# One power for two rows, the tail in another order, and the start of M1's split weights in their tiles

## The chip, the cores and the metric

The kernel runs on one core of one Trainium2 chip. The metric is device time in microseconds; the time of a kernel is the median of its runs. The engines that matter are TensorE (matrix products; the profile keeps its matmuls, PE, and its weight loads, PEld, apart), VectorE (DVE), ScalarE (ACT), GpSimd (POOL) and the DMA queues of SP, POOL and ACT.

## The reference

A decoder of two layers on 512 tokens of 1024 features, in 32-bit floats. Each layer normalises, modulates by shift and scale vectors that come from a condition vector, mixes the tokens (layer 0 with window means, layer 1 with a gated unit), adds the gated result, and then does the same with an MLP of 4096 hidden features and a squared ReLU:

```python
def rmsnorm(x, g):
    y = x * lax.rsqrt(jnp.mean(x * x, axis=-1, keepdims=True) + RMS_EPS)
    return y * g

def sq_relu_mlp(h, w1, w2):
    return jnp.square(jax.nn.relu(h @ w1)) @ w2

for i in range(DEPTH):
    sh1, sc1, g1, sh2, sc2, g2 = jnp.split(c_act @ ada_w[i] + ada_b[i], 6, axis=-1)
    h = modulate(rmsnorm(x, norm_mix_g[i]), sh1, sc1)
    y = pool_mixer(h, ...) if i == 0 else sgu_mixer(h, ...)
    x = x + g1[:, None, :] * y
    h = modulate(rmsnorm(x, norm_mlp_g[i]), sh2, sc2)
    x = x + g2[:, None, :] * sq_relu_mlp(h, mlp_w1[i], mlp_w2[i])
return rmsnorm(x, final_g)
```

## The kernel before

**Precision.** Every large product is made of three matmuls in a reduced 32-bit format: both operands are split into a high part (a copy rounded to the format) and a low part (what is left), and low x high, high x low and high x high are added up in PSUM (`mm3`, L187). `split` (L175) does this for weights: ScalarE writes the high part into a tile `wh` (L180) and VectorE the difference into a tile `wl` (L181). Both tiles come from `wpair` (L172), out of five buffers each that are used in turn. Such a tile is 1088 words long though only 1024 are used, so the used part may begin some words in: `at` is that start, in 4-byte words.

**Rows.** The 512 tokens are four row tiles t = 0 to 3 of 128 tokens. Rows 0 and 1 make up half 0, rows 2 and 3 half 1.

**The MLP.** `mlp` (L670) multiplies matrices by a scheme of seven products of half size, m = 1 to 7, in place of eight. M1, the first matmul of the MLP, is cut into units `("s", (c, j, m))`. `s_prep` (L746) fetches a block of weights, adds a second one to it where m asks for it, and splits it; `s_run` (L772) then runs 24 matmuls with 128 x 128 weights, a slice of `wh` or `wl`, and 256 moving columns, a slice of the split activations. The moving slices begin at multiples of 1024 bytes in their tiles, the weight slices at multiples of 512 bytes plus `at`. `ss_` (L744) is the list of these units in order: 42 in the first MLP (some of whose M1 is done in another way) and 56 in the second, so 98 units and 2352 matmuls. In all of them `at` is `UNDER` = 16 words, 64 bytes (L761). Everywhere else `at` is 0. M2, the second matmul, runs in units `("p", (c, m))` (`p_run`, L860) with the activations as weights and the split weights as moving operand, 512 columns at a time. The very last unit of the kernel is cut finer: row 3 is finished in two blocks of 256 columns (L887).

**Order.** TensorE's instructions are issued as the program lists them: `mlp` goes through `units`, prepares a few units ahead and runs them. On the other engines a list scheduler places the instructions at compile time, by priority (program order, with some blocks raised) and by when its model says that they are ready. Items of kind `"x"` in the list of units are calls that are made at that point.

**End of a sublayer.** `gated` (L946) multiplies a piece of the sublayer's result by the gate, adds it to the row tile `x`, squares the sum on ScalarE and keeps the sum of squares in `sums[t]`, a small tile of one row tile. With the second piece VectorE adds the two partial sums and the epsilon (L960). `rms(t)` (L964) raises that to the power -1/2 on GpSimd (`power`, L257), one instruction of 128 x 1 for each row tile. `normed(hf, i, n)` (L967) scales both row tiles of a half by these roots on ScalarE (L973), transposes them on TensorE (L985) and splits the result. It is called four times: for half 0 and half 1 ahead of layer 1's mixer, and the same ahead of layer 1's MLP. The first of these is an item of the first MLP's list, behind M2's unit (1, 4) (L1055).

**The tail.** `last1` (L1175) ends the second MLP. Rows 0, 1 and 2 are finished by `out_rows` (L1166): the power, two products of 512 columns on VectorE (L1170) and two transfers from SP's queue. Row 3 comes in three pieces; after the third its sum is completed (L962), its power taken, and its four quarters are scaled by ScalarE (L1189) and VectorE (L1191, L1192) and sent off from ACT's and SP's queues.

Of the kernel before, what the change touches and what calls it, by code (L numbers as in the profile page):

```python
# [7 lines left out]
F32 = mybir.dt.float32  # L8
F32R = mybir.dt.float32r
AF = mybir.ActivationFunctionType  # L10
ALU = mybir.AluOpType
# [3 lines left out]
P = 128  # L15
D = 1024
# [4 lines left out]
RMS_EPS = 1e-6  # L21
# [3 lines left out]

LATE = 5

UNDER = 16

LEAD = 4  # L30

# [52 lines left out]
def decoder_kernel(ctx: ExitStack, tc: tile.TileContext, xtok, vecs, rows, fgrow, ada0, adag, ada1, pool_w, w1s, w1f, w1b, w2, w_v, w_u, w_o, wsT, lnp, bs, out):  # L84
    nc = tc.nc
    V, A, G, T = nc.vector, nc.scalar, nc.gpsimd, nc.tensor
# [44 lines left out]
    def slot(tag, shape, name, dt=F32):  # L131

        pool = big if tag in ("P0", "P1", "P2", "P3", "R0", "R1", "R2", "S6", "S7") else late[0]
        return pool.tile(shape, dt, name=name, tag=tag)
# [11 lines left out]
    def X(t):  # L146
        return x_[t // 2][:, t % 2]
# [27 lines left out]
    def split(r, n=1, at=0):  # L175

        h, l = wpair(at)
        for q in range(n):
            c = slice(D // n * q, D // n * (q + 1))
            A.activation(h[:, c], r[:, c], AF.Copy)  # L180
            V.tensor_tensor(l[:, c], r[:, c], f32(h[:, c]), ALU.subtract)  # L181
        return h, l
# [74 lines left out]
    def power(v, n):  # L257

        r = sm.tile([P, n], F32, name="rr", tag=f"rr{n}")
        G.tensor_tensor(r, v, mhalf[:, 0:n], ALU.pow)  # L260
        return r
# [8 lines left out]
    with (  # L270
# [67 lines left out]
        def rms():  # L338
            v0 = sm.tile([P, NT], F32, name="rv4", tag="rv4")
            V.tensor_scalar(v0, ss, RMS_EPS, None, ALU.add)  # L340
            rt.append(power(v0, NT))
# [328 lines left out]
    def mlp(i, extra, units, final):  # L670
# [75 lines left out]
        def s_prep(u):  # L746
            c, j, m = u

            def b(r, n):
                return blk(c, j, r, n)  # L750

            def add(o, r, n):
                G.dma_start(o, w1b[i, 2 * c + j, r, n], accum_op=ALU.add)

            t = b(0, 0)
            if m in (5, 6):
                V.tensor_tensor(t, t, b(*CHAIN[m]), ALU.add)
            if m == 5:
                add(b(0, 1), 1, 1)
            wb = b(1, 1) if m == 3 else b(1, 0) if m == 2 else b(0, 1) if m == 7 else t  # L760
            w = split(wb, 1, UNDER)  # L761
            if m == 6:
                add(t, *CHAIN[4])
            for at in more.get(u, ()):
                blk(*at)
            if spare and (u == ss_[0] or in_gb(c, j, *{2: (1, 0), 3: (1, 1)}.get(m, (0, 0)))):
                blk(*spare[0])
            return w
# [177 lines left out]
    def gated(t, c0, n, src, y=None):  # L946
        tmp = sm.tile([P, S], F32, name="tmp", tag="tmp", bufs=2)[:, 0:n]
        xt = X(t)[:, c0 : c0 + n]
        if y is not None:
            V.tensor_tensor(y, y, src, ALU.add)  # L950
        V.tensor_tensor(tmp, src if y is None else y, gbs[0][:, c0 : c0 + n], ALU.mult)
        V.tensor_tensor(xt, xt, tmp, ALU.add)  # L952
        if t not in sums:
            sums[t] = sm.tile([P, 4], F32, name="sums", tag=f"sums{t}", bufs=1), []
        s, cs = sums[t]
        A.activation(tmp, xt, AF.Square, scale=D**-0.5, accum_out=s[:, len(cs) : len(cs) + 1])  # L956
        cs.append(c0)
        if len(cs) == 2:

            V.tensor_scalar(s[:, 3:4], s[:, 0:1], s[:, 1:2], RMS_EPS, ALU.add, ALU.add)  # L960
        elif len(cs) == 3:
            V.tensor_tensor(s[:, 3:4], s[:, 3:4], s[:, 2:3], ALU.add)  # L962

    def rms(t):  # L964
        return power(sums.pop(t)[0][:, 3:4], 1)

    def normed(hf, i, n):  # L967

        xs = []
        x2 = slot(f"R{hf}", [P, 2, D], "xs") if n else None  # L970
        for r in range(2):
            t = x2[:, r] if n else w4.tile([P, D], F32, name="xs", tag="w4")
            A.activation(t, X(2 * hf + r), AF.Copy, scale=rms(2 * hf + r))  # L973
            xs.append(t)
        c = slice(256 * hf, 256 * hf + 256)
        if (i, n, hf) == (1, 0, 0):
            h_[:] = hparts(["S0", "S1", "S2", "S3"])
        if (i, n, hf) == (1, 1, 0):
            h32[:] = [slot(f"P{j}", [P, 4, S], "h32") for j in range(2)]
            h_[:] = hparts(["S0", "S1", "S2", "S3"])  # L980
        for k in range(0, KD, 2):
            px = bank("px")
            for q in range(2):
                for r in range(2):
                    T.transpose(px[:, 256 * q + P * r : 256 * q + P * r + P], xs[r][:, P * (k + q) : P * (k + q) + P], ident)  # L985
            tt = h32[k // 4][:, k % 4 : k % 4 + 2, c] if i and n else sm.tile([P, 2, 256], F32, name="tt", tag="tmp", bufs=2)
            for q in range(2):
                a, b = scl[i][n][:, k + q : k + q + 1], mod(i, c_sh(n, k + q))
                if q or n:
                    A.activation(tt[:, q], px[:, 256 * q : 256 * q + 256], AF.Identity, bias=b, scale=a)  # L990
                else:
                    V.tensor_scalar(tt[:, q], px[:, 0:256], a, b, ALU.mult, ALU.add)
            if (i, n, hf) != (1, 1, 1):
                parts(H2(k, c), tt)
# [27 lines left out]
    def after(us, at, *what):  # L1022
        n = us.index(at) + 1
        us[n:n] = what
# [27 lines left out]
    us += rest(2, 0)  # L1052
    after(us, ("s", (3, 1, 3)), ("tl", (0,)))
    us += p_units(((3, 2), 0, 0), ((3, 2), 1, 0), ((1, 4), 2, 1), ((1, 4), 3, 1))
    after(us, ("p", (1, 4)), ("x", lambda: normed(0, 1, 0)))  # L1055
    after(us, ("p", (1, 5)), ("x", spread(0, "gain0")))
    mlp(0, ex, us, lambda t, dh, c0, n, src, y: gated(t, S * dh + c0, n, src, y))

# [105 lines left out]
        nc.sync.dma_start(fgb[0], fgrow.rearrange("(o a) -> o a", o=1).to_broadcast([P, D]))  # L1164

    def out_rows(t):  # L1166
        r = rms(t)
        for j in range(2):
            c = slice(S * j, S * j + S)
            V.scalar_tensor_tensor(X(t)[:, c], X(t)[:, c], r, fgb[0][:, c], ALU.mult, ALU.mult)  # L1170
            nc.sync.dma_start(out[t, :, j], X(t)[:, c])
# [3 lines left out]
    def last1(t, dh, c0, n, src, y):  # L1175
        gated(t, S * dh + c0, n, src, y)
        done.append(t)
        if t < NT - 1:
            if done.count(t) == 2:
                out_rows(t)  # L1180
            return
        xt = X(t)
        if done.count(t) == 1:
            V.tensor_tensor(xt[:, S:D], xt[:, S:D], fgb[0][:, S:D], ALU.mult)
        elif done.count(t) == 2:
            V.tensor_tensor(xt[:, 0:256], xt[:, 0:256], fgb[0][:, 0:256], ALU.mult)
        else:
            r = rms(t)
            A.activation(xt[:, S:D], xt[:, S:D], AF.Copy, scale=r)  # L1189
            nc.scalar.dma_start(out[t, :, 1], xt[:, S:D])  # L1190
            V.scalar_tensor_tensor(xt[:, 256:S], xt[:, 256:S], r, fgb[0][:, 256:S], ALU.mult, ALU.mult)  # L1191
            V.tensor_scalar(xt[:, 0:256], xt[:, 0:256], r, None, ALU.mult)  # L1192
            nc.sync.dma_start(out[t, :, 0], xt[:, 0:S])
# [102 lines left out]
```

## Time and profile before

| | |
|---|---|
| three timed runs | 858.62, 863.02 and 864.4 us; median 863.02 |
| profiled execution | 864.85 us, span 863.1 us, mean granted TensorE clock 0.992 |
| instructions | 12746 |
| M1 of the first MLP | about 106 to 226 us |
| M2 of the first MLP | about 226 to 387 us |
| layer 1's mixer | about 387 to 534 us |
| M1 of the second MLP | 534 to 700 us |
| M2 of the second MLP and the tail | 700 to 863 us |

The span runs from the first to the last instruction of the program on the core. In the rows of a view, `out<-in` are tiles by their names in the program, `x` is the count, and what stands in brackets is the engine's idle time before the instruction with the instruction that ended it. A matmul's end is modelled, so the distance from one start to the next says more than its length. Rows of the chain of waits follow the work that ended last back to the start.

### The profile page before, as it was taken

To read this page: it belongs to the slowest core of one execution; us is meant where nothing else is said; L and a number is where in the kernel's file an instruction comes from. 1 tells how busy PE (TensorE), PEld (TensorE's weight loads), DVE (VectorE), ACT (ScalarE), POOL (GpSimd) and SP (SyncE) were. 2 spreads that over 40 slices of the span, in tenths; PEclk is the share of its full clock that TensorE was granted. 3 is DMA by queue.
4 is the path that set the end of the run, shared out by engine and by line. 5 is a ranking of instruction groups with operands and counts; after the bars stand their busy time and mean duration, and the time that the engine had idled before them with its cause. 6 is when DMAs were issued, how large, how long until landed. Compare 5 with 4: busy or idle time off the path is not lost.

```text
span 863.1 us, 12746 instructions
## 1 busy us (share of the span) xinstructions
PE 836.9 (97%) x4895; PEld 737.4 (85%) x4895; DVE 690.0 (80%) x878; ACT 514.9 (60%) x740; POOL 117.9 (14%) x137
## 2 busy tenths in 40 slices
PE   9999999999999999989999999999999999999995
PEld 7878898999978888768888887989999998888884
DVE  6889888988689868786799954788787677976886
ACT  4286776666665655656331436867766676665562
POOL 3010001000133300032010001011000032321000
PEclk9999999999999999989999999999999999999998
DMA  9999868899999989344758733558989699998502
GB/s 350 406 339 325 252 186 238 262 284 276 302 217 173 204 224 253 138 163 169 243 180 292 237 121 104 155 155 195 271 245 259 172 220 245 196 214 221 155 17 82
DMA packets 51652, 188.62 MB, mean 219 GB/s; under 512 B 5740, under 2 KB 5892, under 8 KB 50567
## 3 DMA queue, kind: packets, MB, share of 16 engines
q1 hardware_dynamic: 37090, 133.52, 42.9%
q0 software_dynamic: 14352, 54.02, 32.7%
q8 instruction: 38, 0.62, 0.3%
q10 hardware_dynamic: 148, 0.27, 0.1%
q14 instruction: 24, 0.19, 0.1%
HBM read 181.49 MB, written 6.30 MB: 218 GB/s over the span
## 4 chain that ended last, share of the span: by engine, by line
PE 58%; DVE 19%; DMA 12%; issue 5%; ACT 4%; POOL 1%; SPq 0%; POOLq 0%; DVEq 0%; ACTq 0%
PE pm L874 28%; PE po L193 6%; DVE wl L181 4%; DVE ada L217 3%; PE b211q L193 3%; PE b301q L193 3%; DMA wh<-in_ada 2%; PE b201q L193 2%; PE b311q L193 2%; DMA ada<-in_ada 2%; DVE ada L397 2%; ACT wh L180 1%; PE b111q L193 1%; PE b205q L193 1%; PE b305q L193 1%
## 5 line engine op out<-in xcount | busy, mean ns | idle before, releaser
L874 PE MATMUL pm<-wh,o 128*128 128x512 f32 x864 | 216.1, 392 | 3.8 <-DVE o L638 3.1
L874 PEld LDWEIGHTS pm<-wh,o 128*128 128x128 f32 x864 | 162.4, 189 | 39.6 <-DVE o L638 4.3
L874 PE MATMUL pm<-wl,o 128*128 128x512 f32 x432 | 115.7, 389 | 0.1
L180 ACT ACTIVATE wh<-bt 128x1024 fp32r<-128x1024 f32 x64 | 67.1, 1057 | 51.8 <-PE pm L874 42.1
L874 PEld LDWEIGHTS pm<-wl,o 128*128 128x128 f32 x432 | 81.0, 188 | 17.4 <-DVE wl L181 0.5
L181 DVE TENSOR_TENSOR wl<-bt,wh 128x1024 fp32r<-128x1024 f32 x64 | 77.5, 1218 | 20.1 <-ACT wh L180 20.1
L638 DVE TENSOR_TENSOR o<-g,o 128x1024 fp32r<-128x1024 f32 x56 | 68.2, 1217 | 5.6 <-ACT o L637 5.5
L217 DVE SCALAR_TENSOR_TENSOR ada<-ada,cb 128x1024 f32<-128x1024 f32 x56 | 68.0, 1217 | 3.5 <-DMA ada<-in_ada 3.1
L193 PE MATMUL po<-hb,wh 128*128 128x512 f32 x224 | 69.0, 389 | 0.0
L637 ACT ACTIVATE o<-g 128x1024 fp32r<-128x1024 f32 x56 | 58.7, 1048 | 9.5 <-PE pm L874 8.8
L180 ACT ACTIVATE wh<-b 128x1024 fp32r<-128x1024 f32 x32 | 34.0, 1062 | 37.6 <-PE pm L874 37.6
L853 POOL DMA_DIRECT2D bt<-in_w x48 | 41.5, 894 | 108.6 <-DVE wl L181 86.7
L181 DVE TENSOR_TENSOR wl<-b,wh 128x1024 fp32r<-128x1024 f32 x32 | 39.2, 1224 | 21.3 <-ACT wh L180 21.3
L180 ACT ACTIVATE wh<-raw 128x1024 fp32r<-128x1024 f32 x33 | 35.0, 1060 | 32.8 <-PE pm L874 13.8
L181 DVE TENSOR_TENSOR wl<-raw,wh 128x1024 fp32r<-128x1024 f32 x33 | 40.2, 1221 | 14.3 <-ACT wh L180 14.2
L193 PEld LDWEIGHTS po<-hb,wh 128*128 128x128 f32 x224 | 42.1, 188 | 8.6
L193 PE MATMUL po<-hb,wl 128*128 128x512 f32 x112 | 44.1, 394 | 0.5 <-ACT g L700 0.5
L692 ACT ACTIVATE g<-g 128x512 f32<-128x512 f32 (+1 forms) x72 | 41.2, 601 | 1.2
L193 PE MATMUL po<-wh,gt 128*128 128x512 f32 x128 | 40.5, 393 | 0.3 <-DVE gt L1137 0.2
L193 PE MATMUL po<-wh,hb 128*128 128x512 f32 x128 | 39.9, 390 | 0.0
L797 ACT ACTIVATE g<-g 128x512 f32<-128x512 f32 x42 | 26.2, 624 | 16.1 <-DVE g L789 8.7
L956 ACT ACTIVATE tmp<-x 128x512 f32<-128x512 f32 (+1 forms) x25 | 15.2, 609 | 26.9 <-DVE x L952 26.9
(442 smaller groups left out, 2027.6 us busy)
## 6 DMA issues: line engine op xcount, KB each, us to landing
ada<-in_ada SPq DMA_DIRECT2D x72, 512.0 KB, 4.7
bt<-in_w POOLq DMA_DIRECT2D x48, 512.0 KB, 9.0
bt<-in_w SPq DMA_DIRECT2D x16, 512.0 KB, 6.1
raw<-in_w SPq DMA_DIRECT2D x16, 512.0 KB, 7.1
b<-in_w SPq DMA_DIRECT2D x16, 512.0 KB, 10.0
b<-in_w POOLq DMA_DIRECT2D x16, 512.0 KB, 10.2
wh<-in_ada SPq DMA_DIRECT2D x9, 512.0 KB, 9.9
wl<-in_ada SPq DMA_DIRECT2D x9, 512.0 KB, 10.1
```

Of the source, the lines that this page charges most:

```text
L180: A.activation(h[:, c], r[:, c], AF.Copy)
L181: V.tensor_tensor(l[:, c], r[:, c], f32(h[:, c]), ALU.subtract)
L193: T.matmul(o[:, c], a, b[:, c], start=first and q == 0 and not c.start, stop=last and q == 2 and c.stop is None, **kw)
L217: keep(V.scalar_tensor_tensor(r, r, 1.0, cb, ALU.mult, ALU.mult, accum_out=pmv[i, b][:, j : j + 1]))
L397: V.scalar_tensor_tensor(r, r, 1.0, cb, ALU.mult, ALU.mult, accum_out=out)
L637: A.activation(o[0], a, AF.Copy)
L638: V.tensor_tensor(o[1], a, f32(o[0]), ALU.subtract)
L692: A.activation(t, t, AF.Square)
L797: A.activation(t, t, AF.Relu)
L853: G.dma_start(r, piece(c, *nxt, q), accum_op=ALU.add)
L874: T.matmul(banks[hf], o[a][:, 2 * q + p, hf], w[q][b][:, S * p : S * p + S], start=start and q + n + p == 0, stop=stop and q + n + p == 4, ...
L956: A.activation(tmp, xt, AF.Square, scale=D**-0.5, accum_out=s[:, len(cs) : len(cs) + 1])
```

## The change

**M1's weights.** `UNDER` becomes a tuple, and unit number n of a list takes entry n modulo 7 for both of its tiles: the used part begins 64, 128, 192, 32, 96, 160 or 0 bytes into the tile.

**One power for two rows.** The partial sums of both row tiles of a half lie in one tile `[P, 2, 4]`. `roots(hf)` adds the two partial sums and the epsilon of both rows in one VectorE instruction and takes one power of 128 x 2. Ahead of layer 1's MLP (`one=True`) it keeps a sum and a power for each row, in a tile they share. The sums are no longer added up in `gated` but where the roots are taken. For half 0 ahead of layer 1's mixer the roots are called for behind M2's unit (0, 4) and not in `normed` behind unit (1, 4).

**The tail.** Row 2's `out_rows` is called after row 3's power, and the last of row 3's three squares is made by VectorE in place of ScalarE.

```diff
-UNDER = 16
+UNDER = (16, 32, 48, 8, 24, 40, 0)
...
-            w = split(wb, 1, UNDER)
+            w = split(wb, 1, UNDER[ss_.index(u) % len(UNDER)])
...
-        if t not in sums:
-            sums[t] = sm.tile([P, 4], F32, name="sums", tag=f"sums{t}", bufs=1), []
-        s, cs = sums[t]
-        A.activation(tmp, xt, AF.Square, scale=D**-0.5, accum_out=s[:, len(cs) : len(cs) + 1])
+        pair, cs = sums.setdefault(t // 2, (sm.tile([P, 2, 4], F32, name="sums", tag=f"sums{t // 2}", bufs=1), ([], [])) if t // 2 not in sums else None)
+        s, cs = pair[:, t % 2], cs[t % 2]
         cs.append(c0)
-        if len(cs) == 2:
-
-            V.tensor_scalar(s[:, 3:4], s[:, 0:1], s[:, 1:2], RMS_EPS, ALU.add, ALU.add)
-        elif len(cs) == 3:
-            V.tensor_tensor(s[:, 3:4], s[:, 3:4], s[:, 2:3], ALU.add)
-
-    def rms(t):
-        return power(sums.pop(t)[0][:, 3:4], 1)
-
-    def normed(hf, i, n):
+        o = s[:, len(cs) - 1 : len(cs)]
+        if len(cs) == 3:
+            V.scalar_tensor_tensor(tmp, xt, 1.0 / D, xt, ALU.mult, ALU.mult, accum_out=o)
+        else:
+            A.activation(tmp, xt, AF.Square, scale=D**-0.5, accum_out=o)
+
+    def total(t):
+        s = sums[t // 2][0][:, t % 2]
+        V.tensor_scalar(s[:, 3:4], s[:, 0:1], s[:, 1:2], RMS_EPS, ALU.add, ALU.add)
+        return s
+
+    def roots(hf, one=False):
+        pair = sums.pop(hf)[0]
+        v = sm.tile([P, 2], F32, name="rv", tag="rv2")
+        if one:
+            r = sm.tile([P, 2], F32, name="rr", tag="rr2")
+            for q in range(2):
+                V.scalar_tensor_tensor(v[:, q : q + 1], pair[:, q, 0:1], RMS_EPS, pair[:, q, 1:2], ALU.add, ALU.add)
+                G.tensor_tensor(r[:, q : q + 1], v[:, q : q + 1], mhalf[:, 0:1], ALU.pow)
+            return r
+        V.scalar_tensor_tensor(v, pair[:, :, 0], RMS_EPS, pair[:, :, 1], ALU.add, ALU.add)
+        return power(v, 2)
+
+    def normed(hf, i, n, rr=None):
 
         xs = []
+        rr = roots(hf, n == 1) if rr is None else rr()
...
-            A.activation(t, X(2 * hf + r), AF.Copy, scale=rms(2 * hf + r))
+            A.activation(t, X(2 * hf + r), AF.Copy, scale=rr[:, r : r + 1])
...
-    after(us, ("p", (1, 4)), ("x", lambda: normed(0, 1, 0)))
+    rr = []
+    after(us, ("p", (1, 4)), ("x", lambda: normed(0, 1, 0, rr.pop)))
+    after(us, ("p", (0, 4)), ("x", lambda: rr.append(roots(0))))
...
-        r = rms(t)
+        r = power(total(t)[:, 3:4], 1)
...
-            if done.count(t) == 2:
+            if done.count(t) == 2 and t < 2:
                 out_rows(t)
...
             V.tensor_tensor(xt[:, 0:256], xt[:, 0:256], fgb[0][:, 0:256], ALU.mult)
+            total(t)
         else:
-            r = rms(t)
+            s = sums[1][0][:, 1]
+            V.tensor_tensor(s[:, 3:4], s[:, 3:4], s[:, 2:3], ALU.add)
+            r = power(s[:, 3:4], 1)
+            out_rows(2)
             A.activation(xt[:, S:D], xt[:, S:D], AF.Copy, scale=r)
```

## The prediction

> **What bounds the kernel now.** I read the page first, for the busiest engine and the chain; then the chain in order of time; then TensorE's timeline inside M1, the first matmul of both MLPs; then the windows of M1's two long stretches; last the places that the small edits touch.
>
> ```profile
> PE 836.9 (97%) x4895; PEld 737.4 (85%) x4895; DVE 690.0 (80%) x878; ACT 514.9 (60%) x740; POOL 117.9 (14%) x137
> PE 58%; DVE 19%; DMA 12%; issue 5%; ACT 4%; POOL 1%; SPq 0%; POOLq 0%; DVEq 0%; ACTq 0%
> ```
>
> TensorE is busy for 97% of the span and carries 58% of the chain that ended last. So the question is how fast it works where it never waits.
>
> ```profile
> 187.08 2.83 PE b211q L193 x24
> 267.32 73.50 PE pm L874 x324
> 697.27 2.83 PE b311q L193 x24
> ```
>
> These are rows of the chain in order of time: start, length, matmuls. One M1 unit (`s_run`) is 24 matmuls with 256 moving columns, 2.83 us or 117.9 ns each; from 150 to 222 us and from 576 to 699 us nearly every piece of the chain is such a unit, one behind the other. A matmul of M2 with 512 columns takes 73.50 / 324 = 226.9 ns, so half of it would be 113.4 ns for 256 columns. M1 is some 4 ns above that, and M1 is where the weights' start is changed. The same timeline shows that M1 has two speeds:
>
> ```profile
> 125.78 0.39 PE L193 MATMUL b101q<-hb,wl 128*128 128x256 f32 x1
> 138.25 0.28 PE L193 MATMUL b115q<-as,wl 128*128 128x256 f32 x1
> 140.97 0.28 PE L193 MATMUL b111q<-hb,wl 128*128 128x256 f32 x1
> 147.24 0.39 PE L193 MATMUL b111q<-hb,wl 128*128 128x256 f32 x1 [0.67 <-DVE g L793]
> 150.17 0.28 PE L193 MATMUL b205q<-as,wl 128*128 128x256 f32 x1
> 153.00 0.28 PE L193 MATMUL b201q<-as,wl 128*128 128x256 f32 x1
> 558.95 0.36 PE L193 MATMUL b112q<-hb,wl 128*128 128x256 f32 x1
> 569.14 0.38 PE L193 MATMUL b001q<-as,wl 128*128 128x256 f32 x1 [1.62 <-DVE wl L181]
> 572.63 0.38 PE L193 MATMUL b011q<-as,wl 128*128 128x256 f32 x1 [0.48 <-DVE wl L181]
> ```
>
> Each row is the first matmul of a unit. From 138.25 to 140.97 a unit takes 2.72 us, 113.3 ns a matmul; from 150.17 to 153.00 the same work takes 2.83 us, 117.9 ns. The fast speed begins behind an interruption at 125.78, ends behind one at 147.24, returns about 559 and ends at 572.63; between interruptions it doesn't change. That is 11 of the 98 units (42 in the first MLP, 56 in the second). It isn't a matter of buffers or operands: the seven units from 125.78 to 147.24 go round all five weight buffers, and both kinds of moving operand (`hb`, `as`) occur at both speeds. It is a phase between two streams, the weights that are loaded for the next matmul and the columns that move through the present one, and it stays until something breaks it. The granted clock is 1.00 at both speeds:
>
> ```profile
> 136.00:146.00 10.00, 10.00 (x91) 10.00 (x90) 8.34 (x10) 5.05 (x8) 0.86 (x1) 1.00 0.93 290
> 152.00:222.00 70.00, 70.00 (x596) 70.00 (x596) 63.88 (x85) 47.70 (x64) 6.04 (x7) 1.00 0.90 281
> 576.00:699.00 123.00, 123.00 (x1047) 123.00 (x1046) 94.50 (x103) 85.33 (x116) 12.98 (x15) 1.00 0.84 232
> ```
>
> (Length, PE, PEld, DVE, ACT and POOL busy, clock, DMA share, GB/s.) In the first MLP VectorE is busy for 63.88 of 70 us and the DMA engines for 90%; in the second VectorE for 94.50 of 123. A dearer matmul lands on the end in both; a cheaper one in full only in the second.
>
> **The change part by part.**
>
> *M1's weight starts.* The tuple has seven starts, and 42 and 56 units are 6 and 8 rounds of it, so each start serves 14 units. Moving operands begin at whole kilobytes of their tiles and weight blocks at 512-byte steps plus the start. Today all of M1 is at 64 bytes. The only other place with 256 moving columns in this arithmetic is the last block of the last unit, where both operands have start 0:
>
> ```profile
> 850.48 0.28 PE L193 MATMUL pm<-wl,o 128*128 128x256 f32 x1
> 851.56 0.28 PE L193 MATMUL pm<-wl,o 128*128 128x256 f32 x1
> ```
>
> Nine matmuls lie between these two: 1.08 / 9 = 120.0 ns. So start 0 is 2.1 ns dearer than start 64 at its slow speed. The other five starts have no row; the bounds are 113.3 and 120.0, and further up a rival. I take 128 like 0 (both whole steps of 128 bytes) at 120.0, and 192 like 64 at 117.9. For 32, 96 and 160 I take 117.9, the row of a start that is out of step too. Mean: (5 x 117.9 + 2 x 120.0) / 7 = 118.5. Today's mean: (11 x 113.3 + 87 x 117.9) / 98 = 117.4. The difference of 1.1 ns on 98 x 24 = 2352 matmuls is +2.6 us, all of it on the path. With the three half steps at either bound it is -2.0 or +4.7 us; ScalarE's and VectorE's writes to the shifted tiles keep their length, and should one grow, they wait on TensorE in both stretches.
>
> The Trainium skill speaks against any effect: "SBUF — State Buffer", section "Who interferes with whom", gives TensorE two independent read ports, one for the moving operand and one for weights, and says that PE never waits on anyone. By it the start of the weights costs nothing and this term is 0; the two speeds of one and the same unit, 113.3 and 117.9 ns, don't fit it.
>
> *One power for two rows, before the second layer's first norm.*
>
> ```profile
> L260 POOL TENSOR_TENSOR rr<-sums,mhalf x12: 538/556/4886, 369.5 to 857.4; 128x1 f32<-128x1 f32 x12
> 369.32 1.21 DVE L181 TENSOR_TENSOR wl<-bt,wh 128x1024 fp32r<-128x1024 f32 x1
> 369.48 5.42 POOL L260 TENSOR_TENSOR rr<-sums,mhalf 128x1 f32<-128x1 f32 x2 [42.40 <-DVE sums L960]
> 371.59 2.35 DVE L181 TENSOR_TENSOR wl<-bt,wh 128x1024 fp32r<-128x1024 f32 x2
> 374.40 2.19 ACT L973 ACTIVATE xs<-x,rr 128x1024 f32<-128x1024 f32 x2 [3.95 <-POOL rr L260]
> 375.61 0.47 PE L985 MATMUL px<-ident,xs 128*128 128x128 f32 x1 [2.35 <-ACT xs L973]
> 376.65 3.46 PE L985 MATMUL px<-ident,xs 128*128 128x128 f32 x15 [0.57 <-ACT xs L973]
> ```
>
> A power takes 0.54 to 0.56 us, but the first of this pair took 4.89: it began at 369.48 and ended, with VectorE's unbroken run of tensor-tensor work (369.32 to 373.94), at 374.37. ScalarE waited 3.95 us, TensorE 2.35 + 0.57. This is the stall that the earlier call aims at. But row 1's sum, which the joint power needs, still comes behind ScalarE's second square, in the same place of VectorE's queue (about 369.2), and the second power is not what is waited for: it ended about 374.9 while ScalarE worked on row 0 until 375.5. The joint power would again sit under VectorE's run and end about 374.4. I put it at 0: the power is held by VectorE, not by its own place. Bounds: -2.9 us if it finds a gap before the run, +0.6 if the sum slips behind the run (a sum, 0.2, and the handing over). The same page and section of the skill names that lock: a VectorE instruction with two SBUF inputs contends with a GpSimd one that reads SBUF, and the later one blocks; the trace agrees, 4.89 us against 0.54.
>
> In the other norms two short sums become one, or are made later: 0.21 us of VectorE each (the sum's row in the next fence), on no path that TensorE waits for longest. I cost them at 0; the queue behind them on VectorE is the splits of the next units, which can come 0.2 us earlier or later.
>
> *The tail.*
>
> ```profile
> 852.83 0.21 DVE L960 TENSOR_SCALAR sums<-sums 128x1 f32<-128x1 f32 x1
> 853.76 1.41 DVE L1170 SCALAR_TENSOR_TENSOR x<-x,rr,fgb 128x512 f32<-128x512 f32 x2 [0.72 <-POOL rr L260]
> 855.55 0.41 DVE L951 TENSOR_TENSOR tmp<-pm,gb 128x256 f32<-128x256 f32 x1
> 856.52 0.42 ACT L956 ACTIVATE tmp<-x 128x256 f32<-128x256 f32 x1 [3.04 <-DVE x L952]
> 857.06 0.16 DVE L962 TENSOR_TENSOR sums<-sums 128x1 f32<-128x1 f32 x1 [0.64 <-ACT tmp L956]
> 857.94 0.48 DVE L1191 SCALAR_TENSOR_TENSOR x<-x,rr,fgb 128x256 f32<-128x256 f32 x1 [0.72 <-POOL rr L260]
> 858.35 0.35 DVE L1192 TENSOR_SCALAR x<-x,rr 128x256 f32<-128x256 f32 x1
> 858.72 0.33 SPq L1193 DMA_DIRECT2D out<-x  x1
> ```
>
> Row 2's two products (1.41 us) stand ahead of row 3's last gate at 855.55. If they really move behind row 3's power, the gate starts about 1.3 us earlier, but VectorE has the same work before it is done: what it loses in front it does at the end, and row 2's own two transfers leave SP's queue there, with row 3's behind them. Only the wait for GpSimd (0.72) could be filled: -0.7 us. Against that, four transfers instead of two leave in the last 1.5 us; I allow +0.5. The third square on VectorE instead of ScalarE costs about 0.48 (the 256-column product's row) plus reading the sum, against 0.62 from 856.44 to the sum at 857.06: -0.1. Together -0.1, between -0.8 and +0.5.
>
> *Sum.* +2.6 + 0 + 0 - 0.1 = +2.5 us. The profiled execution took 864.85 us (span 863.1), so 867.35; it lies 1.8 us above the median of the three timed runs, 863.02. On the median's footing: 865.5 us. A difference under 1% (8.6 us) I call no change, which is about what a measurement here can tell.
>
> **The rivals.**
>
> *The change of start breaks the phase (faster).* Of the five interruptions quoted above three left it fast (125.78, 558.95, 569.14) and two slow (147.24, 572.63): about half. If a new start at each unit acts as an interruption does, without its wait, 49 units are fast instead of 11: 38 x 24 x 4.6 ns = 4.2 us. About 1 us of it is lost in the first MLP, whose VectorE is already at 91% and which waited 0.67 us at the end of its fast stretch. -3.3 us: 859.7. It decides as soon as more than some 35 units run fast, for then it outweighs the 2.6 us above. For it: the speed depends on nothing but history. Against: start 0 gave 120.0 in the tail from its first matmuls, so a start has a speed of its own.
>
> *All starts but 64 are free of the conflict (faster).* 87 x 24 x 4.6 ns = 9.6 us, less 1 in the first MLP: 854.5. Against it: the tail.
>
> *Half steps cost double (slower).* A weight block that begins at 32, 96 or 160 bytes may touch one more step of memory and meet the moving columns twice as often. The tail's excess over the fast speed is 6.7 ns; doubled, 126.7 for three starts of seven: mean 122.3, +4.9 ns, +11.5 us: 874.5. Nothing in the trace speaks for or against it.
>
> *The start does nothing.* The speed depends on history alone, and 113.3, 117.9 and 120.0 come from other things than starts; then the small edits are left: 863 us, where the skill's rule of two free ports would put it. The tail's 120.0 is against it.
>
> **How the numbers follow.** Forecast 0.45 (865.5), phase broken 0.22 (859.7), nothing 0.15 (863), half steps double 0.10 (874.5), all free 0.08 (854.5). The likeliest gives the time. 857 to 870.5 leaves out the last two, and takes in the bounds of the half steps (861 to 867.6), of the power (-2.9) and of the tail around the first three. Faster by over 1% (under 854.4) is half of "all free" and a little of the phase: 0.06. Slower by over 1% (over 871.7) is "half steps double" and the upper end of the forecast: 0.10. Within: 0.84.
>
> **What would show it.** In the timeline of the changed kernel the first matmuls of M1's units lie 2.83 us apart for starts 64 and 192 and 2.88 for 0 and 128; the half steps show their own price. Rows of 2.72 in more than 35 units mean the phase rival; 2.72 nearly everywhere, the all-free one; 3.0 at three starts of seven, the doubled one. The first power still ends with VectorE's run, about 5 us after it starts, and TensorE still waits about 2.9 us there. Row 2's two products lie behind row 3's last gate, and the last transfer leaves right behind the last product, as it does now. I am wrong if the M1 term has the other sign, or if the stall at the power goes.

## The result, and the profile after

The changed kernel takes 865.87 us (median of 11 runs, 863.62 to 869.35); the kernel before, run beside it on the same chips, 860.85 us (11 runs, 853.36 to 866.81). The ratio is 1.008, 95% interval 1.0054 to 1.0105: no change by the bound of 1%, and a loss all the same, as the interval lies above 1. The two profiled executions don't show that loss: 863.62 us after, the changed kernel's lowest run, against 864.85 us before, one of the highest of before. The difference between these two traces is therefore not the difference between the kernels, and much of what follows is about that.

Two lines of the page after, engine totals and chain shares:

```profile
PE 836.3 (97%) x4895; PEld 736.8 (85%) x4895; DVE 690.2 (80%) x878; ACT 514.3 (60%) x738; POOL 115.8 (13%) x135
PE 77%; DVE 9%; DMA 7%; issue 3%; ACT 3%; POOL 1%; SPq 0%; DVEq 0%; POOLq 0%; ACTq 0%
```

TensorE is still what the time consists of, now with 77% of the chain against 58%. The chain in order of time (start, length, group, matmuls) shows M1's units one behind the other, so that each one's speed can be read off:

```profile
160.24 2.87 PE b201q L193 x24
163.12 2.86 PE b211q L193 x24
165.98 2.83 PE b201q L193 x24
168.81 2.85 PE b215q L193 x24
171.66 2.83 PE b211q L193 x24
174.48 2.84 PE b215q L193 x24
177.32 2.82 PE b212q L193 x24
180.14 2.87 PE b211q L193 x24
```

The weights of these eight begin 160, 0, 64, 128, 192, 32, 96 and again 160 bytes into their tiles; a row's length divided by 24 gives 119.6, 119.2, 117.9, 118.8, 117.9, 118.3, 117.5 and 119.6 ns a matmul. Over all units (the mean time between the starts of a unit's consecutive matmuls, without the few distances over 150 ns, which hold a wait; a unit is called fast below 115 ns) M1 takes 118.3 ns with 3 units below 115, against 117.3 with 11 in the trace of before: 2352 x 0.93 ns = 2.2 us between the two traces. Next, windows (length, then PE, PEld, DVE, ACT and POOL busy with counts, clock, DMA share, GB/s): of before a stretch of layer 1 in which most matmuls have 512 columns, and of after the first MLP's stretch, which the prediction showed of before, and the same stretch of layer 1:

```profile
412.00:442.00 30.00, 30.00 (x134) 24.85 (x133) 26.11 (x42) 9.74 (x12) 2.00 (x2) 1.00 0.69 223
```

```profile
152.00:222.00 70.00, 70.00 (x593) 70.00 (x592) 63.68 (x84) 48.00 (x64) 6.64 (x8) 1.00 0.89 278
412.00:442.00 30.00, 30.00 (x131) 24.33 (x130) 27.57 (x46) 9.29 (x13) 2.84 (x3) 1.00 0.71 237
```

In the first stretch 593 matmuls fit where 596 did. The second was not in the prediction at all: TensorE never waits in these 30 us and the clock is 1.00 in both, yet three matmuls fewer fit. Their starts say why: 480 matmuls of 512 columns now lie 232.5 ns apart on average, where the others, and all of them before, lie 227.0 apart.

The stall at the second layer's first norm, after (the timeline there: start, length, group, and in brackets the wait before it and its releaser):

```profile
369.04 3.90 POOL L260 TENSOR_TENSOR rr<-rv,mhalf 128x2 f32<-128x2 f32 x1 [43.35 <-DVE rv L976]
370.01 2.35 DVE L181 TENSOR_TENSOR wl<-bt,wh 128x1024 fp32r<-128x1024 f32 x2
372.97 2.19 ACT L986 ACTIVATE xs<-x,rr 128x1024 f32<-128x1024 f32 x2 [3.94 <-POOL rr L260]
374.17 0.33 PE L998 MATMUL px<-ident,xs 128*128 128x128 f32 x1 [2.45 <-ACT xs L986]
375.21 3.03 PE L998 MATMUL px<-ident,xs 128*128 128x128 f32 x13 [0.71 <-ACT xs L986]
```

One power for both rows, 3.90 us instead of 4.89; it began 1.1 us nearer to the end of VectorE's run (372.36 here) and again ends just behind it. ScalarE waits 3.94 us (3.95 before), TensorE 2.45 + 0.71 (2.35 + 0.57 before). And the tail:

```profile
853.27 0.43 DVE L951 TENSOR_TENSOR tmp<-pm,gb 128x256 f32<-128x256 f32 x1
854.19 0.42 DVE L958 SCALAR_TENSOR_TENSOR tmp<-x 128x256 f32<-128x256 f32 x1
854.96 1.05 POOL L260 TENSOR_TENSOR rr<-sums,mhalf 128x1 f32<-128x1 f32 x2 [16.36 <-DVE sums L1205]
856.05 1.41 DVE L1185 SCALAR_TENSOR_TENSOR x<-x,rr,fgb 128x512 f32<-128x512 f32 x2 [1.24 <-POOL rr L260]
857.38 0.48 DVE L1210 SCALAR_TENSOR_TENSOR x<-x,rr,fgb 128x256 f32<-128x256 f32 x1
857.77 0.35 DVE L1211 TENSOR_SCALAR x<-x,rr 128x256 f32<-128x256 f32 x1
858.15 0.33 SPq L1212 DMA_DIRECT2D out<-x  x1
```

Row 3's last gate now stands right behind the last matmul, and row 2's products behind row 3's power, as the change says.

### The profile page after: what moved, and what is told of

Its sections match the earlier page's. It is cut to its first block, busy times and chain, and to the rows that moved or that the text cites. A ratio compares the mean times of both kernels' runs of the same rounds, so it can differ in the third digit from the quotient of the medians.

```text
span 861.9 us, 12735 instructions
## 1 busy us (share of the span) xinstructions
PE 836.3 (97%) x4895; PEld 736.8 (85%) x4895; DVE 690.2 (80%) x878; ACT 514.3 (60%) x738; POOL 115.8 (13%) x135
## 4 chain that ended last, share of the span: by engine, by line
PE 77%; DVE 9%; DMA 7%; issue 3%; ACT 3%; POOL 1%; SPq 0%; DVEq 0%; POOLq 0%; ACTq 0%
PE pm L874 30%; PE po L193 17%; DVE wl L181 3%; PE b211q L193 3%; PE b201q L193 3%; PE b301q L193 3%; PE b311q L193 3%; DMA wh<-in_ada 2%; PE b111q L193 2%; PE b101q L193 1%; PE b315q L193 1%; PE b305q L193 1%; PE b215q L193 1%; PE b205q L193 1%; PE pm L193 1%
## 5 line engine op out<-in xcount | busy, mean ns | idle before, releaser
L193 PEld LDWEIGHTS po<-wh,hb 128*128 128x128 f32 x128 | 24.1, 188 | 5.6
```

Source lines behind the costliest of these rows:

```text
L193: T.matmul(o[:, c], a, b[:, c], start=first and q == 0 and not c.start, stop=last and q == 2 and c.stop is None, **kw)
```

## The experiments

Each was run against the kernel before on the same chip. A table first, of every trace: M1's mean time per matmul and how many of its 98 units are below 115 ns; the time per matmul of the 480 matmuls of 512 columns whose operands the small edits move; whether the granted clock falls in 370 to 385 us and in 485 to 505 us; the profiled run's time, and the median with its number of runs.

| kernel | M1 ns (fast units) | 512 columns, ns | falls | profiled us | median us (runs) |
|---|---|---|---|---|---|
| before | 117.3 (11) | 227.0 | 1st | 864.85 | 860.85 (11), 859.66 over all 100 |
| before_again | 117.1 (16) | 226.9 | both | 866.50 | one run |
| before_third | 114.2 (80) | 227.0 | 1st | 854.87 | one run |
| before_fourth | 114.1 (81) | 227.0 | both | 857.29 | one run |
| after | 118.3 (3) | 232.5 | 1st | 863.62 | 865.87 (11) |
| small_edits | 116.4 (32) | 232.6 | none | 860.97 | 861.05 (12) |
| starts_turn | 118.3 (3) | 227.0 | both | 869.46 | 865.26 (12) |
| start96 | 117.5 (0) | 232.6 | none | 864.58 | 865.17 (12) |
| small_aligned | 115.7 (46) | 227.0 | both | 862.74 | 859.73 (12) |
| before_shifted | 116.0 (41) | 232.6 | none | 860.15 | 860.82 (12) |
| after_aligned | 118.4 (1) | 227.0 | 1st | 862.10 | 866.14 (10) |
| start192 | 117.8 (0) | 227.0 | both | 869.69 | 867.01 (9) |
| starts_fine | 118.5 (0) | 227.0 | both | 866.28 | 866.51 (10) |
| two_starts | 113.9 (86) | 227.0 | both, and at 230 to 250 us | 865.70 | 857.80 (12) |

### The change taken apart: small edits alone, starts alone

The changed kernel with all starts at 64 bytes:

```
-UNDER = (16, 32, 48, 8, 24, 40, 0)
+UNDER = (16,)
```

> The change with all M1 starts back at 64 bytes, so the joint power and the new tail alone. Theory A (the loss is M1's: the turning starts cost the fast speed of 113.3 ns that before has in stretches): the time is that of before, 0 to -1 us (the profiled tail of the change is 0.8 us shorter, from the last matmul to the last transfer), ratio 0.998 to 1.001, and M1 again has stretches at 113.3 ns. Theory B (the small edits cost it): +4 to +6 us, ratio 1.005 to 1.008, with M1's pitch as before.

The kernel before with only the starts turning:

```
-UNDER = 16
+UNDER = (16, 32, 48, 8, 24, 40, 0)
...
-            w = split(wb, 1, UNDER)
+            w = split(wb, 1, UNDER[ss_.index(u) % len(UNDER)])
```

> The kernel before with only the seven starts in turn. Theory A: as the whole change, ratio 1.006 to 1.010, mean M1 pitch 118.2 to 118.5 ns, at most 5 units of 98 at 113.3. Theory B: the M1 part alone would be at most the difference of the two profiled executions' means, 118.3 - 117.3 = 1.0 ns x 2352 = 2.2 us, ratio 1.002 to 1.003.

The changed kernel with all starts at 96 bytes:

```
-UNDER = (16, 32, 48, 8, 24, 40, 0)
+UNDER = (24,)
```

> The change with all M1 starts at 96 bytes, the cheapest of the new starts in the change's trace (116.6 to 118.5 ns by unit, mean 117.2). If a start has a speed of its own: M1 at 116.6 to 117.2 throughout, 1 ns under the slow speed of 64; against before, which has part of its units at 113.3, ratio 0.999 to 1.004. If the speed is a matter of history alone: M1 as in before, both speeds, 113.3 and 117.8.

And the kernel before once more, for its trace:

> The kernel before once more, for its profile. Theory A says that its spread (853 to 867 us) is the number of units at the fast speed: time = 864.9 - 0.108 x (fast units - 11), so an execution at 860 us has about 55 fast units. Theory C (the spread comes from transfers or waits): the number of fast units stays near 11 and the waits of TensorE differ.

The small edits alone: ratio 1.0024 (0.9996 to 1.0052), above theory A's range and below theory B's. The turning starts alone: 1.0049 (1.002 to 1.0077), 865.26 against 860.24 us, between the two theories in time, with M1 as theory A said (118.3 ns, 3 fast units). So by the medians the larger part of the loss is M1's. Start 96 for all units: 1.0061 (1.0034 to 1.0088), above what was expected, with no fast unit, so history alone doesn't set the speed; yet its M1 mean of 117.5 ns is hardly above that of the first trace of before. That is the first sign that 117.3 ns is not what before usually has. The second is the spread: before runs from 854.96 to 866.6 us here, start96 only from 862.91 to 867.57. The second trace of before, 866.50 us, has 16 fast units and two falls of the clock where the first has one, so it decides between neither of its theories.

### Where the tiles lie

The small edits change more than their instructions. Four small tiles of sums (32 bytes each in the allocation) became two, and two new names for pairs of values came with three buffers each: 6 x 32 - 2 x 32 = 128 bytes more, and every tile behind them moved by as much. Among these are all four tiles that hold `hb` in the second layer and two of the four that hold `gt`; the weight tiles `wh` and `wl` lie in front and stayed. Before, both operands of every 512-column matmul of this line began at the same place modulo 256 bytes; after, 480 of them are 128 bytes apart. An unused tile of 128 bytes tells this from the joint power:

```
     sums = {}
+    sm.tile([P, 32], F32, name="pad", tag="pad", bufs=1)
```

Added to the kernel before it moves the tiles by 128 bytes; added to the change it makes the move 256 bytes in all, so the places modulo 256 are those of before. It went into the small edits alone, into the kernel before, and into the whole change:

> The changed kernel with every weight start at 64 bytes (the small edits alone) and one unused tile of 128 bytes among the small tiles. In the traces of the three kernels with the joint power, the new small tiles have moved the tiles named hb and two of the four named gt by 128 bytes, and the 480 matmuls of 512 columns that read them together with an unmoved weight tile take 232.4 to 232.8 ns where the others take 227.0. The unused tile brings them back to the places of before. Theory L (the cost follows where the tiles lie): those matmuls fall back to 227.0 ns, 480 x 5.5 ns = 2.6 us less than the small edits alone (861.05 us): 858.4 us, 0.998 of before. Theory P (the cost follows the moment at which TensorE starts again behind the joint power): the 232 ns stay, and the time stays at 861.0 us. Theory B (other work of the small edits costs it): the time stays at 861.0 us although the matmuls take 227.0 ns.

> The kernel before, with one unused tile of 128 bytes among its small tiles and nothing else, so that hb and two of the gt tiles begin 128 bytes later, as in the changed kernel. Theory L: the 480 matmuls of 512 columns go from 227.0 to 232.5 ns, +2.6 us: 862.8 us, 1.003 of before; of M1's units, those that read the moved tiles have their weights 192 instead of 64 bytes away, which the rows of the small edits price at nothing (117.8 ns both). Theory P: no joint power, so no cost: 860.2 us, and 227.0 ns throughout.

> The changed kernel with its seven starts, and the unused tile of 128 bytes that brings hb and gt back to the places of before. Theory L: 865.9 - 2.6 = 863.3 us, 1.0035 of before, what is left being M1's turning starts; M1's mean is 118.4 ns as in the kernel that has the turning starts alone. Theory P: 865.9 us. If the turning starts were the whole loss (theory A), the time would stay at 865.3 us whatever the tiles' places.

The stretch of 512-column matmuls in before_shifted, and then in small_aligned:

```profile
412.00:442.00 30.00, 30.00 (x131) 24.32 (x130) 26.86 (x48) 8.08 (x10) 4.85 (x4) 1.00 0.69 227
```

```profile
412.00:442.00 30.00, 30.00 (x134) 24.86 (x133) 27.02 (x48) 8.09 (x10) 4.62 (x4) 1.00 0.69 233
```

131 matmuls with the tiles moved and no joint power, 134 with the joint power and the tiles back. As to the matmuls theory L is shown, and P falls: the 232.6 ns follow the tiles' places, at a price of 480 x 5.5 ns = 2.6 us. As to the time it is not shown. before_shifted, 1.0016 (0.9987 to 1.0044), lies 1.2 us above before, and small_aligned, 0.9999 (0.9964 to 1.0034), 1.3 us below the small edits, each half of what L said and within the noise; after_aligned, 1.0074 (1.0045 to 1.0104), is no faster than the changed kernel.

Two things in the traces give time back. One is a wait of TensorE for VectorE's `gt`, here in before_again:

```profile
493.50 0.80 PE L193 MATMUL po<-wh,gt 128*128 128x512 f32 x1 [3.15 <-DVE gt L1137]
```

From the first matmul that reads `hb` to the first that reads `gt` takes 96.1 us in the ten traces with the tiles in their old places and 98.2 us in the four with moved tiles. TensorE so comes later to `gt` and waits less: its waits from there on add up to 0 to 3.85 us in the ten, 2.2 in the mean, and to 0 to 0.7 us in the four, 0.2 in the mean. From the first matmul with `hb` to the last with `gt` all 14 traces take 141.4 to 148.1 us, the ten 145.1 in the mean and the four 144.6, so in them nothing is left of the 2.6 us at the end of this stretch, though with this scatter that isn't shown for the kernels. The other is the clock. The windows behind the stall, before and then small_edits:

```profile
375.00:380.00 5.00, 3.83 (x17) 3.54 (x18) 2.10 (x3) 4.32 (x6) 0.00 (x0) 0.55 0.65 213
380.00:385.00 5.00, 5.00 (x19) 4.00 (x19) 5.00 (x8) 3.40 (x8) 0.00 (x0) 0.77 0.75 225
```

```profile
375.00:380.00 5.00, 4.63 (x28) 4.14 (x29) 4.05 (x6) 4.28 (x7) 0.00 (x0) 1.00 0.71 261
380.00:385.00 5.00, 5.00 (x23) 4.13 (x23) 5.00 (x8) 3.34 (x6) 1.81 (x1) 1.00 0.88 302
```

Behind TensorE's wait the granted clock fell to 0.55 and 0.77 in one trace, which costs (0.45 + 0.23) x 5 = 3.4 us of TensorE's work, and not at all in the other. Of the ten traces with the tiles in their old places all have this fall, and seven have the second one, at 485 to 505 us; of the four with moved tiles one has the first and none the second. Over all runs the mean granted clock is 0.9941 with the tiles moved (47 runs) and 0.9927 otherwise (154 runs, the difference 0.0014 with a standard error of 0.0004): 0.0014 x 860 = 1.2 us given back. The second fall comes in the seven traces in which the waits for `gt` add up to 2.17 us or more, and in no other, so for this one the shorter wait is the likely reason. The first fall depends on how its wait lies in time. All changes of the clock in one trace are whole multiples of 3.41 us apart, and a fall lasts 3.41 or 6.83 us. Here are such steps of 3.41 us, before and then small_edits:

```profile
372.06:375.47 3.41, 1.19 (x6) 0.65 (x4) 1.88 (x2) 1.07 (x2) 2.85 (x2) 1.00 0.21 19
375.48:378.88 3.40, 2.71 (x12) 2.42 (x13) 0.98 (x2) 2.72 (x5) 0.00 (x0) 0.50 0.74 294
```

```profile
370.00:373.40 3.40, 1.89 (x9) 1.23 (x7) 2.52 (x3) 0.27 (x1) 3.09 (x1) 1.00 0.00 0
373.42:376.82 3.40, 1.78 (x14) 1.60 (x15) 0.87 (x2) 3.07 (x4) 0.00 (x0) 1.00 0.86 307
```

In before most of the wait falls into one step, with TensorE busy for 1.19 us, and the next step has half the clock; in the small edits nearly the same wait is shared by two steps, and the clock stays. Between 12 and 840 us of the 14 traces every step at full clock with TensorE busy for at most 1.53 us (20 of them) is followed by half the clock, and none of the 3331 with 1.64 us or more is. Nothing in the traces ties the place of the steps to that of the tiles, so that three of the four traces with moved tiles escape the first fall may be chance. That after_aligned shows no gain fits its clock (0.9919 against 0.9935 of the changed kernel, 1.4 us) and the scatter of ten runs; its time alone doesn't show the 2.6 us.

The Trainium skill, page "TensorE: Matmul & The Clock Gate", Part 1, describes such a gate: half rate is the default, activity lifts it, and an idle window of about 3.4 us brings it back. The lowest clock in a row here is 0.50, which agrees; but a step of 3.41 us need not be idle to bring it, as TensorE was busy for up to 1.53 us of such a step.

### Is 192 the other side of 64?

```
-UNDER = 16
+UNDER = 48
```

> The kernel before with every weight start at 192 bytes instead of 64. In the traces so far a unit of start 64 takes 113.3 or 117.8 ns per matmul, in stretches, and in one stretch of the small edits (from 574 us on) units 64 bytes away are fast while units 192 bytes away are slow. Theory T (the two starts are the two sides of one phase: where 64 is slow, 192 is fast): the 82 to 87 units that are slow in before become fast and its 11 to 16 fast ones slow, some 70 x 0.108 = 7.6 us less: 852.6 us. Theory A (192 has the same two speeds and falls into the slow one for most units): 117.5 ns in the mean, 860 to 861 us, no difference from before.

867.01 us, 1.0085 (1.0052 to 1.0119), the dearest of all. No unit was fast, 98 of 98 lie at 117.6 to 117.9 ns. Theory T falls. Theory A's M1 mean of 117.5 was right, its time wrong by 6 us, because it compared with a trace of before that had few fast units itself.

### Neighbours of 64

```
-UNDER = (16, 32, 48, 8, 24, 40, 0)
+UNDER = (12, 14, 18, 20, 4, 28, 44)
```

> The kernel before with M1's weight starts turning unit by unit through 48, 56, 72, 80, 16, 112 and 176 bytes, so that each start's price shows in 14 units; the prices so far, in ns per matmul: 0 bytes 119.3, 32 118.3, 64 113.3 or 117.8, 96 117.5, 128 118.7, 160 119.9, 192 117.8 and never fast. Theory S (each start has a price of its own, and the turning breaks nothing): neighbours of 64 share its two speeds, so 56, 72 or 80 have some units near 113.3, the others lie between 117.3 and 120; the time is 2352 x (mean of the rows - 116.2) above before, some 862 to 866 us. Theory R (only the 64-byte cell of the start counts): 72, 80 and 112 take 113.3 or 117.8 as 64 does, 16, 48 and 56 take 119.3 as 0 does, 176 takes 118.7 as 128 does: mean 118.2, 864.5 us. Theory A (the turning itself holds every start out of its fast speed): no unit below 115.

866.51 us, 1.0078 (1.0041 to 1.0114). The means by start: 16 bytes 118.5, 48 118.2, 56 117.8, 72 118.5, 80 118.7, 112 119.9, 176 118.2; no unit below 117.5. Theory R falls with start 112, in the same 64 bytes as 64 and the dearest of all. Theory S fails with the neighbours 56, 72 and 80, none of which shares the fast speed. Theory A's forecast came true, but this run alone doesn't show that the turning is the cause: these starts may be slow by themselves.

### What an ordinary execution of before looks like

Two more traces of the kernel before:

> The kernel before, once more, for its trace: does a lower time come with more of M1's units at 113.3 ns? The two traces of before so far have 11 and 16 such units of 98 and mean clocks of 0.992 and 0.991, at 864.85 and 866.5 us, which are among its highest times. Theory F (two states that change from run to run make its spread: the share of M1 at 113.3 ns, 0.108 us a unit, and the dips of the granted clock behind the waits near 372 and 490 us, some 0.86 us for each 0.001 of the mean clock): time = 864.85 - 0.108 x (fast units - 11) - 0.86 x (clock - 0.992)/0.001, within 2 us; at the median of 860 us that is some 25 to 40 fast units, or a clock near 0.996. Theory C (transfers make the spread): the fast units stay at 11 to 16 and the clock at 0.991 or 0.992, whatever the time.

> As the run beside it, one more trace of the kernel before: theory F gives its time within 2 us from its fast units and its clock, 864.85 - 0.108 x (fast units - 11) - 0.86 x (clock - 0.992)/0.001; theory C expects 11 to 16 fast units at any time.

The first MLP's stretch and one of the second MLP's, before_third:

```profile
152.00:222.00 70.00, 70.00 (x620) 70.00 (x619) 65.10 (x88) 48.01 (x65) 6.90 (x8) 1.00 0.90 288
580.00:680.00 100.00, 100.00 (x884) 100.00 (x884) 80.18 (x87) 72.54 (x101) 9.53 (x11) 1.00 0.84 240
```

and the second one in the trace of before that the prediction was made from:

```profile
580.00:680.00 100.00, 100.00 (x851) 100.00 (x850) 81.16 (x89) 70.51 (x96) 10.39 (x12) 1.00 0.84 234
```

620 matmuls where the prediction quoted 596, 884 where it would have found 851, with the same program. The chain of before_fourth says the same by units:

```profile
134.50 2.72 PE b111q L193 x24
137.22 2.72 PE b115q L193 x24
139.94 2.72 PE b111q L193 x24
```

80 and 81 units are fast, against 11 and 16. Theory F's formula gives 864.85 - 0.108 x 69 - 0.86 x 2 = 855.7 us for the first (measured 854.87) and 864.85 - 0.108 x 70 = 857.3 us for the second (857.29). Theory C is out. In these four traces the spread of before is mostly M1's share at the fast speed, which differs between executions by up to 70 units or 7.6 us, and the clock.

### Two starts in turn

```
-UNDER = 16
+UNDER = (16, 48)
...
-            w = split(wb, 1, UNDER)
+            w = split(wb, 1, UNDER[ss_.index(u) % len(UNDER)])
```

> The kernel before with M1's weight starts in turn at 64 and 192 bytes. The runs so far say that only start 64 has the speed of 113.3 ns (11, 16, 80 and 81 of 98 units in four traces of before), that start 192 never has it, and that the units at 64 of the three kernels with seven starts had it in 6 of 42 cases. Open is whether the turning itself carries TensorE out of that speed. Theory T2 (each unit takes its own start's price, and the phase outlives a unit at 192): the 49 units at 64 are fast as often as in before, about half, and the other 49 never: some 24 fast units where before has 48, 24 x 0.108 = +2.6 us, about 862.5 us against 860 of before. Theory A (each change of start throws the phase away): no or next to no unit below 115, 48 x 0.108 = +5.2 us, 865 us.

Both theories fall, on the side that neither had. 86 units are fast, 46 of the 49 at 64 bytes and 40 of the 49 at 192, a start that alone never was:

```profile
152.00:222.00 70.00, 70.00 (x620) 70.00 (x619) 66.15 (x89) 48.77 (x66) 6.90 (x8) 1.00 0.90 290
580.00:680.00 100.00, 100.00 (x884) 100.00 (x883) 82.59 (x91) 70.26 (x97) 9.53 (x11) 1.00 0.87 248
```

Slow units occur only near the waits (at 105 and 108 us, 125 to 138 and 541 to 578 us), and after at most three slow units M1 is fast again, mostly without a wait in between, while with one constant start and the tiles in their old places a slow stretch lasted until the next wait.

How far the weights lie from the moving columns doesn't settle it. In the second MLP of small_edits the moved `hb` puts the weights of its units 192 instead of 64 bytes from the moving columns, while the units with `as` stay at 64. From 574 us on all 20 units with `as` take 113.4 ns and all 24 with `hb` between them 117.8, switching from unit to unit without a wait. In two_starts units 192 bytes apart were fast between units at 64; there it was the weights that had moved.

The median of two_starts is 857.80 us and ten of twelve runs lie between 855.29 and 859.36; the ratio to the 13 runs of before beside it, 857.57 us, is 0.9979 (0.9943 to 1.0015), so it isn't shown to be faster than before. It is 8 us below the changed kernel's 865.87 us, though the two were not run side by side. Its profiled run, 865.70 us, is one of two that lost to the clock:

```profile
240.00:250.00 10.00, 10.00 (x35) 7.96 (x34) 6.29 (x7) 4.13 (x4) 1.72 (x2) 0.73 1.05 224
```

## Why the prediction was right in the time, and where it was not

The forecast, 865.5 us within 857 to 870.5, is 0.4 us from the median of 865.87. Two errors cancelled: the sum, +2.5 us, is half of the difference of the medians (+5.0 us; 6.9 by the ratio), and the footing, the 863.02 us of three runs, lies 2.2 us above the median of eleven. That the time came out so close is luck.

**M1's term, the changed side.** Sized right: 118.5 ns forecast, 118.3 measured. By starts it was right for 64 and 192 (117.9 forecast; 117.3 and 117.5 in starts_turn), 0 (120.0; 119.3), 32 (117.9; 118.4) and 96 (117.9; 117.7), and wrong for 128 (120.0; 118.6) and 160 (117.9; 119.6), which nearly offset each other.

**M1's term, the side of before.** This is the step that failed: "Today's mean: (11 x 113.3 + 87 x 117.9) / 98 = 117.4". It was right for that one execution. The prediction had seen that the phase is left by chance at each interruption, and then took one draw of it for the kernel. ("It stays until something breaks it" holds for this kernel; small_edits shows units of both speeds in turn without a wait.) Four traces of before have 11, 16, 80 and 81 fast units, a mean of 115.7 ns, and by that the term is (118.3 - 115.7) x 2352 = +6.1 us instead of +2.6. The warning was in the times: 858.62 to 864.4 us in three runs of one program, while the profiled one was above all of them.

**The joint power, 0.** Right, for the reason given: GpSimd's power ends with VectorE's run of two-input operations, and TensorE's two waits there are 2.45 and 0.71 us in the changed kernel against 2.35 and 0.57 before, +0.2 us. Undoing only the tiles' move leaves the small edits at 0.9999 of before.

**What the power brought along.** Missing: the places of its tiles, +2.6 us in matmuls, of which some 1.2 came back through the clock by the runs, and by the traces up to all of it through the wait for `gt` and the clock. The prediction treated the distance between weights and moving columns as a matter of M1's starts alone ("Moving operands begin at whole kilobytes of their tiles") and didn't ask whether the tiles stay.

**The tail, -0.1.** Right: from the last matmul's start to the span's end it is 8.94 to 9.12 us in the five traces with the new order and 9.16 to 9.24 in the nine without, -0.2 us. The wait for GpSimd that I hoped to see filled grew instead, to 1.24 us, as two powers now stand one behind the other.

**The sum anew.** M1 +6.1, tiles +2.6 - 1.2, power +0.2, tail -0.2: +7.5 us, or +6.1 us if the tiles cost nothing in the end. The ratio's interval is +4.6 to +9.0 us. The M1 entry rests on four traces that fall into two groups, so it may be off by some us.

**The rivals.** "Half steps cost double" fell: no start took more than 119.9 ns in the mean. "All starts but 64 are free" fell: seven starts, and 96 or 192 alone, have next to no fast units. "The start does nothing" fell with starts_turn: at a granted clock of 1.00 one and the same matmul took 113.3 to 119.9 ns, and 227.0 or 232.5, by where its operands lie and by history. The Trainium skill says on the page "SBUF — State Buffer", section "Who interferes with whom", that TensorE's two read ports are independent and PE waits on nobody; the term of 0 that the prediction drew from this doesn't hold here, and no run shows whether the ports are the cause. "The change of start breaks the phase" fell for these seven starts, 3 fast units, but with 64 and 192 in turn a change of start does bring the fast speed: 86 units.

**What stays open.** Which steps from one start to the next lead into the fast phase (64 to 192 and back does; the seven in this order don't), why a constant 192 never gets there, why units 192 bytes apart are slow in small_edits and fast in two_starts, and whether the moved tiles have a part in the first fall of the clock.

## What to carry to other kernels

Before a term is worked out from "the mean of today", look whether the trace holds stretches of two speeds, and if it does, take several traces: a difference between two profiled executions may be one draw of each. When an edit adds or drops even a small tile, compare where all later tiles begin, as operands that are read together may move against each other. And when a stall is priced, ask what the clock does behind it: here two waits of 2.4 and 0.6 us could cost another 3.4.

## What the runs showed of the hardware

- A matmul of 256 columns whose weights begin 64 bytes off takes 113.3 or 117.8 ns in one and the same program; one speed can last from one wait of TensorE to the next (147 to 222 us), and the waits can change it. It can also change from unit to unit without a wait (small_edits from 574 us on: 20 units 64 bytes apart at 113.4 ns, 24 units 192 apart between them at 117.8).
- With the starts in turn at 64 and 192 bytes units at both starts become fast (86 of 98 below 115 ns); at 192 alone none is; the dearest starts, 112 and 160, take 119.9 and 119.6.
- A matmul of 512 columns takes 227.0 ns when both operands begin at the same place modulo 256 bytes, and 232.5 when they are 128 apart, whether the moved tile is loaded as weights or streamed through.
- The granted clock changed in steps of 3.41 us. Between 12 and 840 us of 14 traces it fell to 0.50 behind each of the 20 steps with TensorE busy for at most 1.53 us and behind none of the 3331 with 1.64 us or more (before 12 us two traces have a fall that this doesn't cover); each fall lasted 3.41 or 6.83 us, a loss of 1.7 or 3.4 us of TensorE's work. In 11 of the 14 traces one stood at the same place, at 370 to 385 us.
- Four traces of before took 854.87, 857.29, 864.85 and 866.50 us with 80, 81, 11 and 16 fast units; for the others of its 100 runs, 852.86 to 867.17 us, the units aren't known.
